# Interleaved rotary embedding: plain fp32 transfers on two queues, casts on ScalarE, tiles of eight positions

## The chip, the core and the metric

The kernel runs on one core of a Trainium2 chip. The metric is the device time of one execution in microseconds; the median of several runs is compared. A profile is one such execution with every instruction and every DMA packet recorded.

The core has several engines, each with a queue of its own that runs in order. VectorE (DVE in the profile) does elementwise work on two tensors, ScalarE (ACT) copies, casts and scales, GpSimd (POOL) is used here only to issue transfers, and SyncE (SP) issues transfers too. Data move between the memory outside (HBM) and the memory on the core (128 partitions) through 16 DMA engines. An engine that issues a transfer doesn't wait for it; whoever needs the data waits on a semaphore.

## What is computed

`x` has shape (8, 2048, 16, 64) in fp32: batch, position, head, element. Neighbouring elements form pairs, and each pair is turned by an angle that depends on the position and on the pair's place in the head:

```
x1, x2 = x[..., 0::2], x[..., 1::2]
out[..., 0::2] = x1 * cos - x2 * sin
out[..., 1::2] = x1 * sin + x2 * cos
```

`cos` and `sin` have shape (2048, 32): one value for each position and pair, the same for every batch and head. Input and output are 67.1 MB each. The arithmetic may be done in bf16.

## The kernel before

A tile holds 128 partitions x K = 4 positions x 16 heads x 64 elements, that is 4096 elements in each partition. The sequence is cut into G = 4 groups of 512 positions. Neighbouring positions lie in one partition, so each partition's part of a tile is one run of 16 KB in HBM. There are 8 batches x 4 groups = 32 tiles; the outer loop runs over groups, the inner one over batches, so that a group's tables serve eight tiles.

All tiles on the core are bf16. The transfers themselves cast: the load (L73) reads fp32 and writes bf16, and the store (L86) reads bf16 and writes fp32. Both are issued on GpSimd's queue, in program order.

The tables are loaded in fp32 by eight small transfers on SP's queue (L50, L51). For each group, `build_tables` (L53 to L64) spreads them on ScalarE to full tiles of 4096 bf16 elements: for each of the four positions one copy of cos, doubled for both elements of a pair and repeated for the 16 heads (L61), and two of sin, with a plus sign for even places (L62) and a minus sign for odd ones (L63).

For each tile VectorE then runs three operations over 4096 elements: `qt = x * s_tab` (L78), `pt = x * c_tab` (L79), and `pt = pt + swap(qt)` (L84), where the swap is done by the access pattern, which reads each pair of `qt` backwards.

A framework orders the instructions and sets the waits. `xt` has five buffers, `qt` and `pt` four each, the tables three. A load waits until VectorE has read its buffer's earlier tile; the multiply into `pt` waits until the earlier store from that buffer has landed.

Of the kernel before, what the change touches and what calls it, by code (L numbers as in the profile page):

```python
# [2 lines left out]

# [4 lines left out]


@with_exitstack  # L10
def kernel(
    ctx: ExitStack,
    tc: tile.TileContext,
    x: bass.AP,
    cos: bass.AP,
    sin: bass.AP,
    out: bass.AP,
):
    nc = tc.nc
    fp32 = mybir.dt.float32  # L20
    bf16 = mybir.dt.bfloat16
    mult = mybir.AluOpType.mult
    add = mybir.AluOpType.add

    B, S, H, D = x.shape
    P = 128
    K = 4
    G = S // (P * K)
    D2 = D // 2
    HD = H * D  # L30
    W = K * HD
    ntiles = B * G

    TAIL_SPLIT = 0

    x_t = x.rearrange("b (g p k) h d -> (b g) p (k h d)", p=P, k=K)
    out_t = out.rearrange("b (g p k) h d -> (b g) p (k h d)", p=P, k=K)
    cos_g = cos.rearrange("(g p k) c -> g p (k c)", p=P, k=K)
    sin_g = sin.rearrange("(g p k) c -> g p (k c)", p=P, k=K)

    consts = ctx.enter_context(tc.tile_pool(name="consts", bufs=1))
    tabpool = ctx.enter_context(tc.tile_pool(name="tabpool", bufs=3))
    xpool = ctx.enter_context(tc.tile_pool(name="xpool", bufs=5))
    qpool = ctx.enter_context(tc.tile_pool(name="qpool", bufs=4))
    opool = ctx.enter_context(tc.tile_pool(name="opool", bufs=4))

    cos_sb = consts.tile([P, G, K, D2], fp32)
    sin_sb = consts.tile([P, G, K, D2], fp32)
    for g in range(G):
        nc.sync.dma_start(out=cos_sb[:, g], in_=cos_g[g])  # L50
        nc.sync.dma_start(out=sin_sb[:, g], in_=sin_g[g])  # L51

    def build_tables(g):  # L53
        c_tab = tabpool.tile([P, W], bf16, name="c_tab")
        s_tab = tabpool.tile([P, W], bf16, name="s_tab")
        c_dst = c_tab.rearrange("p (k h i j) -> p k h i j", k=K, h=H, i=D2, j=2)
        s_dst = s_tab.rearrange("p (k h i j) -> p k h i j", k=K, h=H, i=D2, j=2)
        for k in range(K):
            c_src = cos_sb[:, g, k : k + 1, :].to_broadcast([P, H, D2, 2])
            s_src = sin_sb[:, g, k : k + 1, :].to_broadcast([P, H, D2])  # L60
            nc.scalar.copy(out=c_dst[:, k], in_=c_src)  # L61
            nc.scalar.copy(out=s_dst[:, k, :, :, 0], in_=s_src)  # L62
            nc.scalar.mul(out=s_dst[:, k, :, :, 1], in_=s_src, mul=-1.0)  # L63
        return c_tab, s_tab  # L64

    tile_idx = 0
    for g in range(G):
        c_tab, s_tab = build_tables(g)
        for b in range(B):
            i = b * G + g  # L70

            xt = xpool.tile([P, W], bf16)
            nc.gpsimd.dma_start(out=xt, in_=x_t[i])  # L73

            qt = qpool.tile([P, W], bf16)
            pt = opool.tile([P, W], bf16)

            nc.vector.tensor_tensor(out=qt, in0=xt, in1=s_tab, op=mult)  # L78
            nc.vector.tensor_tensor(out=pt, in0=xt, in1=c_tab, op=mult)  # L79
            q_swap = dataclasses.replace(  # L80
                qt, offset=qt.offset + 1, ap=[qt.ap[0], [2, W // 2], [-1, 2]]
            )
            pt3 = pt.rearrange("p (a j) -> p a j", a=W // 2, j=2)
            nc.vector.tensor_tensor(out=pt3, in0=pt3, in1=q_swap, op=add)  # L84

            nc.gpsimd.dma_start(out=out_t[i], in_=pt)  # L86
            tile_idx += 1


# [1 line left out]
_INS = ['x', 'cos', 'sin']  # L91
_OUTS = [((8, 2048, 16, 64), 'float32')]


# [23 lines left out]
```

## Time and profile before

| | |
|---|---|
| median of 12 runs | 323.04 us (322.67 to 323.32) |
| the profiled execution | 323.09 us |
| its span, first to last instruction | 321.3 us |
| store issues: from issue to landing, median | 12.6 us, 32 of them |
| load issues: from issue to landing, median | 22.7 us, 32 of them |
| last multiply, add and store begin | 303.2, 305.5, 308.1 us |

Busy time counts instructions that compute. The DMA row gives, for each of 40 equal slices of the span, the busy share of the 16 DMA engines in tenths; the row below it gives the bytes they moved, counted at the destination. Where a transfer casts, its source has twice or half as many bytes.

### The profile page before, as it was taken

Reading aid. Unit: us, or ns where it says so; the run is one execution under the profiler, and the core shown is the slowest. Engines: PE = TensorE matmul, PEld = TensorE weight load, DVE = VectorE, ACT = ScalarE, POOL = GpSimd, SP = SyncE. Lnnn points to the kernel's source line nnn. Section 1 sums busy time; section 2 is a strip of 40 time slices with the busy share of each in tenths; the row PEclk is TensorE's granted clock in tenths of the full one; section 3 lists DMA queues with packets and bytes.
Section 4 is the critical chain, followed back from the end, with each engine's and each line's share of the span. In section 5 each row is a group of like instructions: output and inputs, shape, how many; then the busy total and the mean of one; then the engine's idle time right before and its main releaser. Section 6 shows DMA issues by size and latency. Waiting matters only on the chain.

```text
span 321.3 us, 304 instructions
## 1 busy us (share of the span) xinstructions
DVE 213.1 (66%) x96; ACT 36.9 (11%) x49; POOL 34.4 (11%) x68
## 2 busy tenths in 40 slices
DVE  0799887601999901999900999920899920899930
ACT  8698100000820000000000000000000000000000
POOL 3010100400010030010030001030001030000100
DMA  7999999999999999999999999999999999999994
GB/s 137 214 220 214 347 329 432 424 428 249 217 215 392 428 443 255 212 212 390 433 432 262 213 219 377 428 424 286 217 217 357 426 441 289 217 212 343 445 432 169
DMA packets 10371, 101.21 MB, mean 315 GB/s; under 512 B 1153, under 2 KB 2177, under 8 KB 2177
## 3 DMA queue, kind: packets, MB, share of 16 engines
q0 software_dynamic: 9216, 100.67, 101.6%
q1 hardware_dynamic: 1152, 0.52, 0.8%
q14 instruction: 3, 0.02, 0.0%
HBM read 67.63 MB, written 67.11 MB: 419 GB/s over the span
## 4 chain that ended last, share of the span: by engine, by line
DVE 43%; DMA 32%; issue 15%; POOL 3%; ACT 2%; POOLq 0%; DVEq 0%
DMA xt<-in_x_dram 24%; DVE pt L84 17%; DVE qt L78 14%; DVE pt L79 13%; DMA out_dram<-pt 7%; POOL out_dram L86 1%; POOL xt L73 1%; ACT c_tab L61 1%; ACT s_tab L62 1%; ACT s_tab L63 1%; DMA cos_sb<-in_cos_dram 1%; POOLq L113 0%; POOLq L86 0%; DVEq L78 0%
## 5 line engine op out<-in xcount | busy, mean ns | idle before, releaser
L78 DVE TENSOR_TENSOR qt<-xt,s_tab 128x4096 bf16<-128x4096 bf16 x32 | 73.1, 2287 | 80.0 <-DMA xt<-in_x_dram 80.0
L79 DVE TENSOR_TENSOR pt<-xt,c_tab 128x4096 bf16<-128x4096 bf16 x32 | 73.1, 2286 | 14.5 <-ACT c_tab L61 10.3
L84 DVE TENSOR_TENSOR pt<-pt,qt 128x4096 bf16<-128x4096 bf16 x32 | 73.1, 2286 | 0.2
L86 POOL DMA_DIRECT2D out_dram<-pt x32 | 17.1, 534 | 260.5 <-DVE pt L84 260.5
L73 POOL DMA_DIRECT2D xt<-in_x_dram x32 | 17.2, 560 | 13.5 <-DVE qt L78 11.0
L62 ACT CAST s_tab<-sin_sb 128x512 bf16<-128x512 f32 x16 | 12.2, 762 | 52.1 <-DVE qt L78 48.1
L61 ACT CAST c_tab<-cos_sb 128x1024 bf16<-128x1024 f32 x16 | 16.2, 1022 | 0.5 <-DMA cos_sb<-in_cos_dram 0.5
L63 ACT ACTIVATE s_tab<-sin_sb 128x512 bf16<-128x512 f32 x16 | 12.2, 760 | 0.0
L61 ACT ACT_TABLE_LOAD x1 | 1.3, 1283 | 0.7 <-PEq L102 0.7
L102 POOL MEMSET const-float32-0.0<- 128x1 f32 x1 | 0.1, 98 | 0.2 <-issue 0.2
L102 POOL MEMSET const-bfloat16-1.0<- 128x1 bf16 x1 | 0.1, 101 | 0.0
L102 POOL MEMSET const-float32-1.0<- 128x1 f32 x1 | 0.1, 98 | 0.0
L102 POOL MEMSET const-uint8-127<- 128x1 uint8 x1 | 0.1, 98 | 0.0
## 6 DMA issues: line engine op xcount, KB each, us to landing
out_dram<-pt POOLq DMA_DIRECT2D x32, 2048.0 KB, 12.6
xt<-in_x_dram POOLq DMA_DIRECT2D x32, 1024.0 KB, 22.7
cos_sb<-in_cos_dram SPq DMA_DIRECT2D x4, 64.0 KB, 13.0
sin_sb<-in_sin_dram SPq DMA_DIRECT2D x4, 64.0 KB, 17.6
```

The source lines that it names most:

```text
L61: nc.scalar.copy(out=c_dst[:, k], in_=c_src)
L62: nc.scalar.copy(out=s_dst[:, k, :, :, 0], in_=s_src)
L63: nc.scalar.mul(out=s_dst[:, k, :, :, 1], in_=s_src, mul=-1.0)
L73: nc.gpsimd.dma_start(out=xt, in_=x_t[i])
L78: nc.vector.tensor_tensor(out=qt, in0=xt, in1=s_tab, op=mult)
L79: nc.vector.tensor_tensor(out=pt, in0=xt, in1=c_tab, op=mult)
L84: nc.vector.tensor_tensor(out=pt3, in0=pt3, in1=q_swap, op=add)
L86: nc.gpsimd.dma_start(out=out_t[i], in_=pt)
L102: nc = _bacc.Bacc("TRN2", target_bir_lowering=False, num_devices=1)
```

## The change

- Transfers no longer cast. `x` is loaded as fp32 on SP's queue and the result is stored as fp32 on ScalarE's queue (Activation). GpSimd has no part any more.
- K is 8, so G = 2 and there are 16 tiles of 8192 elements in each partition, 32 KB in fp32. Five such tiles (`NX`) are held. The result is written back into the tile from which x came, and the store reads it there. When the last piece of tile i has been widened, the load of tile i + 5 into the same buffer is put on SP's queue, where it waits for the store to land.
- Computing goes in pieces of four positions (4096 elements): `halve` casts a piece to bf16 on ScalarE, `rotate` does the three VectorE operations, in place where it can, and `widen` casts back to fp32 on ScalarE. `halve` runs one piece ahead of `rotate`. There are three buffers for the halved piece and one for `qt`.
- The first tile is loaded and worked in pieces of 1, 1, 2 and 4 positions, the last one in 4, 2, 1 and 1, and the last one is stored so as well.
- The tables are compact: one value for each position and element of a head, without the 16 heads. They are built once for the whole sequence, by three VectorE instructions, from two transfers in place of eight. The multiplies repeat a table row over the heads through their access pattern (a step of 0). The table transfers come after the four loads of tile 0 on SP's queue.
- The order of instructions is the program's own (`manual_schedule`).

The core of the diff:

```diff
-    K = 4
+    K = 8
+    NX = 5
...
-        nc.sync.dma_start(out=cos_sb[:, g], in_=cos_g[g])
-        nc.sync.dma_start(out=sin_sb[:, g], in_=sin_g[g])
...
-            nc.scalar.copy(out=c_dst[:, k], in_=c_src)
-            nc.scalar.copy(out=s_dst[:, k, :, :, 0], in_=s_src)
-            nc.scalar.mul(out=s_dst[:, k, :, :, 1], in_=s_src, mul=-1.0)
...
-            nc.gpsimd.dma_start(out=xt, in_=x_t[i])
-            nc.vector.tensor_tensor(out=qt, in0=xt, in1=s_tab, op=mult)
-            nc.vector.tensor_tensor(out=pt, in0=xt, in1=c_tab, op=mult)
-            nc.vector.tensor_tensor(out=pt3, in0=pt3, in1=q_swap, op=add)
-            nc.gpsimd.dma_start(out=out_t[i], in_=pt)
...
+    first_runs = [(0, 1), (1, 2), (2, 4), (4, 8)]
+    last_runs = [(0, 4), (4, 6), (6, 7), (7, 8)]
...
+    def load(i):
+        g, b = groups[i]
+        tiles[i] = xpool.tile([P, K, HD], fp32, name="xt")
+        for k0, k1 in load_runs(i):
+            nc.sync.dma_start(out=tiles[i][:, k0:k1], in_=x_t[b, g, :, k0:k1])
+
+    def halve(j):
+        i, k0, k1 = pieces[j]
+        halved[j] = hpool.tile([P, 4, HD], bf16, name="xh", bufs=3)
+        nc.scalar.copy(out=halved[j][:, : k1 - k0], in_=tiles[i][:, k0:k1])
+
+    def rotate(j):
...
+        qt = hpool.tile([P, 4, HD], bf16, name="qt")
...
+                ap=[a.ap[0], [D, nk], [0, H], [1, D]],
...
+        nc.vector.tensor_tensor(out=rows(qt), in0=rows(xh), in1=tab(s_tab), op=mult)
+        nc.vector.tensor_tensor(out=rows(xh), in0=rows(xh), in1=tab(c_tab), op=mult)
...
+        nc.vector.tensor_tensor(out=xh3, in0=xh3, in1=q_swap, op=add)
...
+    def widen(j):
+        i, k0, k1 = pieces[j]
+        nc.scalar.copy(out=tiles[i][:, k0:k1], in_=rotated.pop(j)[:, : k1 - k0])
+        g, b = groups[i]
+        for r0, r1 in store_runs(i):
+            if r1 == k1:
+                nc.scalar.dma_start(out=out_t[b, g, :, r0:r1], in_=tiles[i][:, r0:r1])
+        if k1 == K and i + NX < n:
+            load(i + NX)
+
+    with tc.manual_schedule():
+        load(0)
+        nc.sync.dma_start(out=cos_sb, in_=cos_t)
+        nc.sync.dma_start(out=sin_sb, in_=sin_t)
+        for i in range(1, NX):
+            load(i)
...
+        nc.vector.tensor_copy(out=s2[:, :, 0], in_=sin_flat)
+        nc.vector.tensor_scalar_mul(s2[:, :, 1], sin_flat, -1.0)
+        nc.vector.tensor_copy(
+            out=c_tab.rearrange("p g k (i j) -> p (g k i) j", j=2),
+            in_=cos_sb.rearrange("p g c -> p (g c)").to_broadcast([P, G * K * D2, 2]),
+        )
+        halve(0)
+        for j in range(len(pieces)):
+            if j + 1 < len(pieces):
+                halve(j + 1)
+            rotate(j)
+            widen(j)
```

## Prediction

> **What bounds the kernel now.** I read the profile's page from the top: busy times, then the 40 slices, then the DMA queues.
>
> ```profile
> span 321.3 us, 304 instructions
> DVE 213.1 (66%) x96; ACT 36.9 (11%) x49; POOL 34.4 (11%) x68
> ...
> DMA  7999999999999999999999999999999999999994
> GB/s 137 214 220 214 347 329 432 424 428 249 217 215 392 428 443 255 212 212 390 433 432 262 213 219 377 428 424 286 217 217 357 426 441 289 217 212 343 445 432 169
> ...
> q0 software_dynamic: 9216, 100.67, 101.6%
> q1 hardware_dynamic: 1152, 0.52, 0.8%
> ...
> HBM read 67.63 MB, written 67.11 MB: 419 GB/s over the span
> ```
>
> No engine is busy for more than 66% of the span, but the 16 DMA engines stand at 9 in every slice except the first and the last. The GB/s row alternates between about 216 and 430 because it counts bytes at the destination: a load reads 16 KB of fp32 per packet and writes 8 KB of bf16, a store the reverse. Counted on the wide side, both are the same. The windows view over pure stretches says so (us, busy of DVE, ACT, POOL, clock, DMA share, GB/s):
>
> ```profile
> 125.00:145.00 20.00, 16.97 (x8) 0.00 (x0) 1.08 (x2) 1.00 1.04 216
> 150.00:170.00 20.00, 11.32 (x6) 0.00 (x0) 4.25 (x8) 1.00 1.06 432
> 250.00:265.00 15.00, 9.15 (x5) 0.00 (x0) 3.71 (x7) 1.00 1.05 428
> ```
>
> Loads: 2 x 216 = 432 GB/s. Stores: 428 to 432. So the kernel is bound by moving 67.11 MB in and 67.11 MB out, 134.22 MB, and DVE's 80 us of waiting for `xt` (L78) are the other side of that. The chain of waits gives DVE 43% and DMA 32%; I don't take the DVE part for the bound, since the DMA engines run full beside it.
>
> The ends, from 0.2 us windows and the timeline:
>
> ```profile
> 1.60:1.80 0.20, 0.00 (x0) 0.20 (x1) 0.20 (x1) 1.00 0.07 20
> ...
> 2.60:2.80 0.20, 0.00 (x0) 0.20 (x1) 0.20 (x1) 1.00 4.04 348
> ...
> 316.80:317.00 0.20, 0.00 (x0) 0.00 (x0) 0.00 (x0) 1.00 0.25 82
> 317.00:317.20 0.20, 0.00 (x0) 0.00 (x0) 0.00 (x0) 1.00 0.00 0
> ```
>
> The first byte (a table) moves at about 1.75, the x loads start in earnest at 2.6, and the last 16 KB packet starts just before 317.0, so data ends about 317.5 and 3.8 us of closing follow. From 2.6 to 317.5 are 314.9 us. The table packets share that time: 0.8% of 321.3 = 2.6 us of all engines. The rest, 312.3 us, moves 134.22 MB at 429.8 GB/s. That includes the turns between loading and storing.
>
> **What the change does, part by part.**
>
> *Bytes.* fp32 loads and stores move the same 134.22 MB of HBM traffic. Since the wide side set the pace before, dropping the cast from the DMA saves nothing by itself. It doubles the bytes on the SBUF side, from half-loaded to fully loaded, which no row here shows.
>
> *Rate.* Packets go from 16 KB to 32 KB and from one queue to two. Bounds: unchanged, 429.8 GB/s, gives 134.22/429.8 = 312.3 us; the ceiling of 435.2 GB/s that the Trainium skill states ("DMA: Bandwidth & Descriptors", Where 436 GB/s comes from) gives 308.4 us. Below: a loss, next paragraph. I take 432, what pure stretches already reach: 310.7 us, a gain of **1.6 us**.
>
> The same page has a figure that speaks against the change: in its section "iDMA fabric", a plain load stream issued from SP with 4 KiB rows runs alone at 408.7 GB/s. By it the data would take 328.4 us. The case's rows show 432 with casting packets whose wide side is 16 KB. If the page's shortfall is a cost for each row (4096 B at 27.2 GB/s is 150.6 ns, at 408.7/16 it is 160.4, so some 10 ns), 32 KB rows make it less than 1%; if it belongs to uncast HWDGE streams as such, it stays. The nearer row here is the packet size, so I side with 432 and keep 408.7 for the range.
>
> *Start.* SP issues its first DMA at 0.74 before and its first byte moves at 1.75. The first thing on SP is now a load of x, so the x data start at 1.75, not 2.6: **0.85 us** gained. Each SP issue took 0.43 us (the eight table issues), and the smallest new load, 0.52 MB, takes 1.2 us to move, so issuing stays ahead.
>
> *Tables.* 1024 rows of 512 B become 512 rows of 1 KB. Below, 0.52 MB at 432 is 1.2 us; above, the 2.6 us of now. The packets are the same few nanoseconds of fixed cost each, so half of the excess of 1.4 goes with half of them: I take 1.9, **0.7 us** gained, whatever place in the queue they have.
>
> *ScalarE.* Removed: 48 table instructions (36.9 us busy with the table load). Added: 64 casts' worth, two for each half tile of 4096 elements.
>
> ```profile
> L61 ACT CAST c_tab<-cos_sb 128x1024 bf16<-128x1024 f32 x16 | 16.2, 1022 | 0.5 <-DMA cos_sb<-in_cos_dram 0.5
> L62 ACT CAST s_tab<-sin_sb 128x512 bf16<-128x512 f32 x16 | 12.2, 762 | 52.1 <-DVE qt L78 48.1
> L78 DVE TENSOR_TENSOR qt<-xt,s_tab 128x4096 bf16<-128x4096 bf16 x32 | 73.1, 2287 | 80.0 <-DMA xt<-in_x_dram 80.0
> L84 DVE TENSOR_TENSOR pt<-pt,qt 128x4096 bf16<-128x4096 bf16 x32 | 73.1, 2286 | 0.2
> ```
>
> 1024 contiguous elements take 1022 ns. Four times that is 4.1 us, an upper bound; with the fixed part of 186 ns of "ScalarE: Activation LUTs" (What ACT_TABLE_LOAD costs) taken out three times, 3.5 us, an estimate; I take 3.6. A tile of 8 positions needs four: 14.4, with one store issue of 0.45 and waits some 15.5 us. The DMA needs 2 x 4.19 MB / 432 = 19.4 us for a tile. So ScalarE has 3.9 us to spare in each tile and its casts would have to reach 4.6 us to become the bound.
>
> *VectorE.* The same three operations over the same elements, 3 x 2.2 us (the pitch in the timeline) = 6.6 for each half tile, 13.2 a tile, against 19.4. New is the table operand with a repeated 64-element row. L84 already reads its swapped operand in runs of two and takes 2286 ns like the contiguous L78, so I cost it at nothing. The three table instructions (512, 512 and 1024 fp32 elements) move to DVE: between 0.6 us each (the DVE rate of L78) and 1.2[...], about 2.5 us at the head, before the first store only.
>
> *Does the DMA queue ever run dry?* Head: five loads at 9.7 us keep the engines busy to 1.75 + 1.9 + 48.5 = 52 alone. Tables land at about 15 (four runs of tile 0 come first), table instructions to 17.5, then the four pieces of tile 0 go through halve, rotate, widen in turn: store 0 goes out at about 36. From then on loads and stores share. At half rate each, a store lands every 19.4 us (55, 75, 94, ...) and releases the load of the tile five further on; load 4 lands at about 67, when load 5 has been waiting since 57. A tile takes about 21 us from its landing to its store; five tiles x 19.4 = 97 us for a buffer's turn leave 76 for a load and a store in the queues. About two of each wait at any time, so SP's wait for a store's landing (only later loads stand behind it on SP) and the store issue behind widening on ACT (the next halve stands behind it, 0.45 us) are covered. If that cover were gone, each missing load would idle the engines for up to 9.7 us.
>
> Tail: load 15 is issued when store 10 lands, near 249, and lands near 281, with some 3.4 tiles of stores (33 us) still to move; tile 15's compute ends about 300. So stores stay queued to the end, and the last piece, 0.52 MB, is long in the queue. I keep the 3.8 us of closing.
>
> **Sum.** 1.75 + 1.9 + 310.7 + 3.8 = 318.15 us of span, 3.15 below 321.3. The profiled execution took 323.09 beside its span of 321.3, so 1.8 us lie around it: **319.9 us**. Its 323.09 is 0.05 above the median of 323.04, so no correction.
>
> **Rivals.**
>
> *Two fp32 queues move less than one casting queue* (the slower side). Place: the 270 us in which each engine alternates between 32 KB loads and stores, with SBUF's side at full load. For: no row shows it; the page's 408.7. Against: the turns between loading and storing are already inside the 429.8 and cost at most 312.3 - 310.7 = 1.6 us. Price: at 420 (the lowest 5 us windows show 419) 319.6 us, so 328.8 in all with the other 9.25; at 408.7, 337.6. It decides below 134.22/(321.3 - 1.75 - 1.9 - 3.8) = 427.7 GB/s: a loss of 0.5% against 429.8 undoes everything. Chance 0.20.
>
> *A compute engine becomes the bound.* If the repeated table row halves the DVE rate, two multiplies of 4.4 and an add of 2.2 make 11 us for each half tile, 352 us plus a head of 17.5 and a tail of about 6 with what lies around: some 377 us. L84 speaks against it; on ScalarE the 3.9 us of slack do. Chance 0.05.
>
> *No difference*: packets and queues leave the rate at 427 to 428.5, so that the head's gain is spent in the transfers: 323 us. For it: the engines are already full; against it: it is a narrow band between the two larger cases. Chance 0.07.
>
> The forecast, 319.9, has 0.68. Its own range is 316.6 (435.2 GB/s and 1 us less closing) to 322.4 (429.8 GB/s gives 321.5, and 0.9 at the ends). A measurement can tell about 0.2%, 0.65 us. The range, with about 1 in 10 left out on each side, reaches into the first rival: 316.5 to 331 (417 GB/s). Faster 0.68, same 0.07, slower 0.25.
>
> **What would show it.** The DMA row at 9 throughout; destination GB/s near 432 in every slice, where it alternated before; first x packet before 2 us; ACT some 235 us and DVE some 215 us busy, both under 75%; halved tiles of 4096 at 3.6 us; table multiplies still at 2.29 us. I am wrong if the GB/s row sits under 427.7 with the engines full, if slices fall below 9 after the head, or if either multiply takes more than 3 us.

## The result and the profile after

The changed kernel takes **318.67 us** (median of 7 runs, 318.57 to 318.83; an eighth run on record, which this median leaves out, took 319.06) against 322.96 us before (29 runs, 322.67 to 323.32). The ratio is 0.9867, 95% interval 0.9858 to 0.9876: 1.3% faster. The forecast was 319.9, 1.0% faster. The profiled execution took 318.59 us; 1.8 us lie around its span, as before.

The page of the changed kernel, first its top:

```profile
span 316.8 us, 352 instructions
DVE 223.2 (70%) x111; ACT 230.0 (73%) x73; POOL 0.2 (0%) x4
...
DMA  8999999999999999999999999999999999999997
GB/s 312 420 459 401 459 397 434 426 455 405 463 397 463 397 460 410 451 434 427 451 410 459 405 455 405 455 410 455 430 430 451 410 430 428 426 432 439 442 414 302
...
q1 hardware_dynamic: 3712, 67.63, 50.1%
q10 hardware_dynamic: 2736, 67.11, 49.1%
...
HBM read 67.63 MB, written 67.11 MB: 425 GB/s over the span
```

The DMA row is full as before, and the GB/s row no longer alternates between 216 and 430: nothing casts on the way, so source and destination have the same bytes. ScalarE went from 11% to 73% busy, and the row shows no cost of it: the DMA engines stay at 9 in all slices but the first and the last. The groups by shape of the same kernel (busy us, mean ns, idle time ahead of them):

```profile
L75 ACT CAST xh<-xt 128x4096 bf16<-128x4096 f32 x30 | 108.1, 3603 | 50.7 <-DMA xt<-in_x_dram 45.4 <-ACT xt L105 5.4
L105 ACT CAST xt<-xh 128x4096 f32<-128x4096 bf16 x30 | 108.1, 3602 | 2.1 <-DVE xh L100 1.8
L94 DVE TENSOR_TENSOR qt<-xh,s_tab 128x4096 bf16<-128x4096 bf16 x30 | 68.8, 2292 | 56.6 <-ACT xh L75 55.8
```

A cast of 4096 elements takes 3.60 us, and the multiply with a repeated table row takes 2292 ns where the full table took 2287: the repetition costs nothing that can be seen.

The two ends, in windows of 0.2 us (columns as before):

```profile
1.40:1.60 0.20, 0.00 (x0) 0.20 (x1) 0.00 (x0) 1.00 0.00 0
1.60:1.80 0.20, 0.00 (x0) 0.20 (x1) 0.00 (x0) 1.00 0.47 82
...
315.20:315.40 0.20, 0.00 (x0) 0.00 (x0) 0.00 (x0) 1.00 0.10 41
315.40:315.60 0.20, 0.00 (x0) 0.00 (x0) 0.00 (x0) 1.00 0.00 0
```

The x data start at 1.7, where before they started at 2.6. By the packet records the last packet ends at 315.55, and only **1.3 us** follow to the end of the span at 316.81. Before, the last packet ended at 317.55, and 3.8 us followed to 321.32. That closing is the largest single piece of the gain, and the prediction had kept it unchanged. It is visible in the sequencer rows, first of the kernel before, then of the changed one (instruction, count, shortest/median/longest ns, first and last start):

```profile
L113 POOLq DRAIN  x3: 40/93/12466, 308.1 to 321.1; - x3
```

```profile
L158 POOLq DRAIN  x3: 34/41/75, 0.7 to 316.6; - x3
```

Before, GpSimd's drain begins after its last store issue at 308.1 and lasts 12.5 us, to 320.6: 3.0 us past the end of the last packet. From its end to the end of the span there are another 0.8 us. In the changed kernel GpSimd has issued nothing and its longest drain takes 75 ns.

### The profile page after: what moved, and what is told of

Same layout as the page of the kernel before. It is cut to its first block, busy times and chain, and to the rows that moved or that the text cites. A ratio compares the mean times of both kernels' runs of the same rounds, so it can differ in the third digit from the quotient of the medians.

```text
span 316.8 us, 352 instructions
## 1 busy us (share of the span) xinstructions
DVE 223.2 (70%) x111; ACT 230.0 (73%) x73; POOL 0.2 (0%) x4
## 4 chain that ended last, share of the span: by engine, by line
DMA 62%; ACT 26%; DVE 4%; issue 3%; another core or an unknown queue 2%; SPq 1%; ACTq 1%
DMA xt<-in_x_dram 31%; DMA out_dram<-xt 28%; ACT xt L105 14%; ACT xh L75 12%; DMA sin_sb<-in_sin_dram 4%; DVE xh L95 1%; DVE xh L100 1%; DVE qt L94 1%; SPq L70 1%; ACTq L109 1%; DVE s_tab L121 0%; SPq L115 0%; DVE s_tab L122 0%; ACTq L105 0%
## 5 line engine op out<-in xcount | busy, mean ns | idle before, releaser
L75 ACT CAST xh<-xt 128x4096 bf16<-128x4096 f32 (+2 forms) x36 | 116.1, 3224 | 66.8 <-DMA xt<-in_x_dram 61.4
L105 ACT CAST xt<-xh 128x4096 f32<-128x4096 bf16 (+2 forms) x36 | 116.0, 3223 | 14.7 <-DVE xh L100 14.4
L94 DVE TENSOR_TENSOR qt<-xh,s_tab 128x4096 bf16<-128x4096 bf16 (+2 forms) x36 | 74.0, 2055 | 71.2 <-ACT xh L75 70.3
L100 DVE TENSOR_TENSOR xh<-xh,qt 128x4096 bf16<-128x4096 bf16 (+2 forms) x36 | 74.0, 2055 | 1.2
L95 DVE TENSOR_TENSOR xh<-xh,c_tab 128x4096 bf16<-128x4096 bf16 (+2 forms) x36 | 74.0, 2055 | 1.2
L123 DVE CAST c_tab<-cos_sb 128x1024 bf16<-128x1024 f32 x1 | 0.7, 684 | 0.0
```

The costliest lines, as they stand in the source:

```text
L75: nc.scalar.copy(out=halved[j][:, : k1 - k0], in_=tiles[i][:, k0:k1])
L94: nc.vector.tensor_tensor(out=rows(qt), in0=rows(xh), in1=tab(s_tab), op=mult)
L95: nc.vector.tensor_tensor(out=rows(xh), in0=rows(xh), in1=tab(c_tab), op=mult)
L100: nc.vector.tensor_tensor(out=xh3, in0=xh3, in1=q_swap, op=add)
L105: nc.scalar.copy(out=tiles[i][:, k0:k1], in_=rotated.pop(j)[:, : k1 - k0])
L123: nc.vector.tensor_copy(out=c_tab.rearrange("p g k (i j) -> p (g k i) j", j=2), in_=cos_sb.rearrange("p g c -> p (g c)").to_broadcast([P, ...
```

## The experiments

All compute the whole result. "Closing" is the time from the end of the last packet to the end of the span.

**1. Who makes the closing: the last store on GpSimd's queue.**

```diff
-                nc.scalar.dma_start(out=out_t[b, g, :, r0:r1], in_=tiles[i][:, r0:r1])
+                eng = nc.gpsimd if i == n - 1 and r1 == K else nc.scalar
+                eng.dma_start(out=out_t[b, g, :, r0:r1], in_=tiles[i][:, r0:r1])
```

> The changed kernel with only its very last store (512 KB) issued from GpSimd's queue in place of ScalarE's. Theory A (the changed kernel gained 2.5 us because its last data are followed by 1.3 us of closing where the kernel before needed 3.8, and that belongs to a last store from GpSimd's queue): 321 to 322 us, closing 3.5 to 4.5 us. Theory B (the closing belongs to the use of GpSimd's queue anywhere in the kernel): the same here, 321 to 322. Theory C (the prediction's: the closing is no part of it, the gain is in the rate): 318.7 within 0.5.

Measured: 318.79 us (318.64 to 319.64), closing 1.2 us. That a last store from GpSimd's queue makes the long closing by itself has fallen. Its drain ended 0.4 us after its last packet; in the kernel before it was 3.0 us. What differs is how much was issued there: 1 transfer against 64.

**2. The table loads on GpSimd's queue.**

```diff
-        nc.sync.dma_start(out=cos_sb, in_=cos_t)
-        nc.sync.dma_start(out=sin_sb, in_=sin_t)
+        nc.gpsimd.dma_start(out=cos_sb, in_=cos_t)
+        nc.gpsimd.dma_start(out=sin_sb, in_=sin_t)
```

> The changed kernel with only its two table loads issued from GpSimd's queue, at the head. Theory A (last store decides the closing): 318.7 within 0.5, closing near 1.3 us. Theory B (any use of the queue): 321 to 322, closing near 3.8. Theory C: 318.7 within 0.5.

Measured: 320.70 us (319.51 to 321.02), closing 1.3. The closing is short, so mere use of the queue doesn't make it long. But the time missed all three expectations. In its profile (319.5 us) the transfers ran dry near the end: 0.56 of the DMA engines' time from 312 to 313 and 0.13 from 314 to 315, because the last piece was widened only by 314.1 (by 312.3 in the changed kernel). Experiment 5 is on why it is so late.

**3. All x loads on GpSimd's queue.**

```diff
-            nc.sync.dma_start(out=tiles[i][:, k0:k1], in_=x_t[b, g, :, k0:k1])
+            nc.gpsimd.dma_start(out=tiles[i][:, k0:k1], in_=x_t[b, g, :, k0:k1])
```

> The changed kernel with all its x loads issued from GpSimd's queue, stores still from ScalarE's. In the kernel before, GpSimd's closing drain ended 2.7 us after the last landing with 64 transfers issued there, in the one with 8 positions 1.3 us with 32, and 0.1 us with 1. Theory A (the drain costs some 0.04 us for each transfer issued on that queue, and it only shows when the queue's last transfer is the kernel's last): closing 1.1 to 1.4 us as in the changed kernel, time 318.7 to 320.0 (the loads start up to 0.9 us later). Rival (any use of that queue costs the long closing): 321 or more. The rate in the middle stays at 433 if the queue that issues makes no difference.

Measured: 326.47 us (326.25 to 326.97), closing 1.4. On the closing the theory holds: 22 transfers were issued on GpSimd, and its drain was over at 317.5, before the last store packets ended at 323.2, so nothing shows at the end. From the end of the last packet of GpSimd's queue to the end of its drain it took 0.4 us with 1 transfer, 0.6 with 2 (experiment 2), 1.3 with 22, 1.8 with 32 (experiment 7) and 3.0 with 64: about 0.4 us and **0.04 us for each transfer**. The 22 here don't cast, the 32 and the 64 do, so the cast isn't the cause. Nearly every transfer has 144 packets here, so it may be the packets that are counted. On the rate the expectation was wrong. First this kernel, then the changed one:

```profile
60.00:260.00 200.00, 139.34 (x61) 143.76 (x42) 6.83 (x13) 1.00 1.00 426
```

```profile
60.00:260.00 200.00, 145.90 (x64) 150.34 (x43) 0.00 (x0) 1.00 1.01 434
```

With loads on GpSimd's queue beside stores on ScalarE's, the full engines moved 426 in place of 434 GB/s. By the packet records of this window it is the loads that lose: a 32 KB load packet took 1253 ns in the mean against 1214 in the changed kernel, with the same median of 1213, as 151 of 1296 took over 1.3 us; a store packet took 1216 against 1213. Why stays open, and so does how much of it GpSimd's queue makes. A rival is not ruled out: as the loads start late here, the tables are the first to move, and in experiment 6 that order alone brings the window to 431.

**4. What the packet size is worth: tiles of 4 positions.** First with ten tiles held, the same bytes; then with six.

```diff
-    K = 8
+    K = 4
-    NX = 5
+    NX = 10
-    first_runs = [(0, 1), (1, 2), (2, 4), (4, 8)]
-    last_runs = [(0, 4), (4, 6), (6, 7), (7, 8)]
+    first_runs = [(0, 1), (1, 2), (2, 4)]
+    last_runs = [(0, 2), (2, 3), (3, 4)]
-        runs = first_runs if i == 0 else last_runs if i == n - 1 else [(0, 4), (4, 8)]
+        runs = first_runs if i == 0 else last_runs if i == n - 1 else [(0, K)]
```

> The changed kernel with tiles of 4 positions (16 KB packets) and ten tiles held, so that the same bytes are held. In the trace of the changed kernel plain packets of 4, 8, 16 and 32 KB take 159, 309, 611 and 1213 ns, that is 8.4 ns on top of 27.2 GB/s whatever their size. Theory A (fixed cost of a packet): 4096 more packets over 16 engines x 8.4 ns = 2.2 us more, 320.6 to 321.2. Rival (packets overlap as the casting ones of before did, so their size is worth nothing): 318.7 within 0.5. A tile of half the size also means twice the waits; if those starved the queues the DMA row would fall below 9.

Measured: 329.93 us (329.88 to 329.97), slower than the kernel before. The middle says what the packets cost, the end says something else. The window from 60 to 260 us, and the DMA row:

```profile
60.00:260.00 200.00, 129.28 (x57) 130.12 (x37) 0.00 (x0) 1.00 1.01 431
```

```profile
DMA  7999999999999999999999999999999999977678
```

431 GB/s against 434 in the changed kernel: the engines are as full, and packets of 16 KB carry some 0.5% less (431.1 against 433.1 when a packet that lies across an edge of the window counts by its share). But after 290 us they run dry. The waits of this kernel name a cause that has nothing to do with packets:

```profile
ACT xh L75 <- DMA out_dram<-xt: 18.2, 4, 12.3
```

A halving, which needs loaded data only, sat behind a store issue. In the trace all transfers share eight semaphores, loads and stores alike, and a store that is held goes out within 0.1 us of the landing of the transfer that had its semaphore before. The store issued at 234.76 has the semaphore of a store that landed at 234.68. The next one, whose cast had ended at 242.3, has that of a load issued at 234.74; the load landed at 263.65, and the store went out at 263.72. With six tiles held (`NX = 6`):

> Tiles of 4 positions as in the run with ten held, but only six held. That run took 329.9 us: its middle ran at 431 GB/s, but from 290 us on its DMA row fell to 5 to 8, because ScalarE's store issues waited for a transfer semaphore (there are eight, taken in turn, and with ten loads ahead the one whose turn it is belongs to a load still queued), and the halving behind them waited too. Theory A (shared semaphores): with fewer loads ahead the waits go and the time is 320.0 to 321.0, which is the packets' price alone. Rival (half tiles as such are too small to keep the queues filled): 325 or more with the DMA row below 9 at the end.

Measured: 320.28 us (320.21 to 320.31), the DMA row at 9 to the end, and the wait for `out_dram` gone. So holding fewer tiles is some 9.6 us faster, and half tiles cost 1.6 us against 318.67. About 0.3 us of this is the tables, whose rows halve with the tile: 1024 packets of 28.6 ns against 512 of 46.8, over 16 engines.

**5. Why the last tile lands so late: load it whole.** The timeline of the changed kernel shows when its runs landed (start, length, what, and in brackets how long the engine waited and for what):

```profile
287.94 1.90 ACT L75 CAST xh<-xt 128x2048 bf16<-128x2048 f32 x1 [1.93 <-DMA xt<-in_x_dram]
...
298.87 1.04 ACT L75 CAST xh<-xt 128x1024 bf16<-128x1024 f32 x1 [5.53 <-DMA xt<-in_x_dram]
...
307.97 1.04 ACT L75 CAST xh<-xt 128x1024 bf16<-128x1024 f32 x1 [6.25 <-DMA xt<-in_x_dram]
```

```diff
-        return first_runs if i == 0 else last_runs if i == n - 1 else [(0, K)]
+        return first_runs if i == 0 else [(0, K)]
```

> The changed kernel with the last tile loaded as one transfer (32 KB packets) in place of runs of 4, 2, 1 and 1 positions; its compute and stores stay in pieces. In the changed kernel the four runs landed at about 288, 299 and 308 us, where 281 had been predicted. Theory A (the DMA engines take one packet from each queue in turn, so packets of 16, 8 and 4 KB get 1/3, 1/5 and 1/9 of the rate beside stores of 32 KB): the whole tile lands by 295, the stores stay queued to the end, and the time is 318.0 to 318.6. Rival (the loads are late because the store before them landed late; the size of the packets doesn't matter): the landing stays at 300 or later, and the time is 319 or more, since no piece can start early.

Measured: **318.42 us** (318.23 to 318.52; the changed kernel 318.57 to 318.83), the lowest median here, 0.25 us below the changed kernel's. That difference is not clear of the noise: against the kernel before, the ratios are 0.9846 to 0.9872 here and 0.9858 to 0.9876 there. What is clear is the landing. The first piece of the last tile now waits for the whole of it, and still:

```profile
281.60 3.60 ACT L75 CAST xh<-xt 128x4096 bf16<-128x4096 f32 x1 [4.76 <-DMA xt<-in_x_dram]
```

The whole tile is there at 281.6, 26 us ahead of the last run of the version in pieces. The packet records of the changed kernel fit one packet from each queue in turn, so that a 4 KB packet waits for a store packet of 32 KB each time. The tile before landed at 260.0 us (median of its 16 closing packets), the runs of 4, 2 and 1 positions at 274.5, 286.7 and 297.6. So 2.10, 1.05 and 0.52 MB took 14.5, 12.2 and 10.9 us, that is 145, 86 and 48 GB/s: 1/3, 1/5 and 1/9 of 433. Cutting the last load so that the tail starts early made it start late. It cost little, because 30 us of stores were queued; in experiment 2 pieces that came 1.8 us later left the engines dry.

**6. The head: tables first, tile 0 whole.** A version with both edits on top of experiment 5, then each alone.

```diff
-        load(0)
         nc.sync.dma_start(out=cos_sb, in_=cos_t)
         nc.sync.dma_start(out=sin_sb, in_=sin_t)
+        load(0)
...
-        return first_runs if i == 0 else [(0, K)]
+        return [(0, K)]
```

> The changed kernel with the tables loaded first and the first and last tile loaded as one transfer each. 704 packets fewer in the loads at 8.4 ns over 16 engines are 0.4 us; the tables' place moves no bytes. Theory (only bytes, packets and the two ends count): 317.9 to 318.5, first store some 8 us earlier. Rival (the small first runs are needed to get going): 319 or more, with the DMA row below 9 in the first slices.

Measured: 321.11 us (320.40 to 323.97). Wrong: slower, and with a spread that no kernel above shows.

> The kernel with the last tile loaded whole (318.4 us), with one more edit: the table loads stand ahead of tile 0 on SP's queue, tile 0 still in four runs. The version that had both this and tile 0 loaded whole took 321.1 us with a spread of 3.6 us between its runs, and its 16 DMA engines ended up to 2 us apart. Theory A (the tables at the very start make the loss): 320 to 322 with a wide spread. Rival (loading tile 0 in one piece makes it): 318.2 to 319.

Measured: 326.39 us (325.27 to 327.63), worse than both expectations.

> The kernel with the last tile loaded whole, with tile 0 loaded whole as well and the tables behind it. Theory A (the tables at the very start made the loss of the version with both): 318.0 to 318.6, 384 packets fewer being worth 0.2 us. Rival (tile 0 in one piece made it): 320 or more with a wide spread.

Measured: 318.64 us (318.36 to 318.88). So the tables' place makes the loss: 8.0 us with tile 0 in runs, 2.5 us with tile 0 whole (321.11 against 318.64). The runs of tile 0 alone make no clear difference (318.42 and 318.64), but behind the tables they go with 5.3 us more. The DMA row of the version with the tables first:

```profile
DMA  7999999999999999999999999999999999995995
```

It drops in the slice from about 292 to 300. Each transfer ends with 16 packets of 4 bytes, as many as there are DMA engines, so the time between the first and the last of them shows how far apart the engines are. In this version the last loaded tile's lie between 281.9 and 292.3 us, in the version of experiment 5 between 279.2 and 281.2: some engine had fallen some 10 us behind, and the waiting tile held up the rest. The lag was not all made at the start. It was 3.0 us when tile 0 had landed, 5.3 at the fourth tile and grew from there to 10.4; in experiment 5 it was 0.5, 1.9 and 2.0. In the two versions with the tables first, single table packets of 1 KB took up to 313 and 516 ns. Behind tile 0 none took more than 61 in the changed kernel and in experiment 5, but one took 195 in experiment 1, which lost next to nothing. What makes an engine fall behind is open.

**7. 32 KB packets in the kernel before, still casting.**

```diff
-    K = 4
+    K = 8
-    tabpool = ctx.enter_context(tc.tile_pool(name="tabpool", bufs=3))
+    tabpool = ctx.enter_context(tc.tile_pool(name="tabpool", bufs=1))
-    qpool = ctx.enter_context(tc.tile_pool(name="qpool", bufs=4))
-    opool = ctx.enter_context(tc.tile_pool(name="opool", bufs=4))
+    qpool = ctx.enter_context(tc.tile_pool(name="qpool", bufs=1))
+    opool = ctx.enter_context(tc.tile_pool(name="opool", bufs=3))
```

> The kernel before with tiles of 8 positions (32 KB on the wide side), still casting in the transfers on GpSimd's queue; one buffer for each table and for qt, three for pt. Theory A (casting packets of 16 KB overlap each other, so their fixed cost is mostly hidden): 322.0 to 323.3. Rival (as in the prediction, the packet size brings the rate from 429.8 to 432 or more): 320.5 to 321.5. If the single buffers starve the queue, the DMA row drops below 9 and the run says nothing on the packets.

Measured: 327.86 us (327.52 to 328.18). As a whole it says nothing on packets, since the queue starved. The busy rows of VectorE and DMA show where:

```profile
DVE  0069996009999930098998299920098899199910
...
DMA  8999999999969699999999999999999999999996
```

The two slices with 6 lie at 90 to 98 and 106 to 114 us. VectorE is full there, and its stores go out 13.1 us apart (82.1, 95.3 and 108.4), where one store takes 9.7 at 433 GB/s; the next loads were issued only at 117.8, behind these stores in GpSimd's order. It isn't the single table buffers: the second group's tables are built from 153 to 172 us, and VectorE waits 1.5 us for them. Where it didn't starve it does. Counting bytes of the wide side from the packet records in full stretches (200 to 250 us after the first load packet): before 431.3 GB/s, this kernel 433.1, the changed kernel 433.2, tiles of 4 positions 431.3. In these four kernels the packet size goes with the rate; with or without a cast in the transfer, on one queue or two, it is the same. So the expectation that casting packets hide their cost was wrong.

**8. How many tiles must be held.** `NX = 3` and `NX = 2` in place of 5.

> The changed kernel with three tiles held in place of five. A tile takes some 21 us from its landing to its store; three tiles at 19.4 us each leave 37 us for a load and a store in the queues, which take 9.7 us each alone and 19.4 each when they share. Theory (the bytes set the time as long as a transfer is queued): just covered, 319 to 323, with the DMA row at 8 or 9. Rival (cover is lost as soon as less than one load waits behind the one that runs): 326 or more.

> The same with two tiles held. A buffer's turn is then load 9.7 + compute 21 + store 9.7 + some 3 us of waits, 43 us for two tiles, against 38.8 us of transfers: the buffers become the bound. Theory: 16 tiles x 21.7 us, 345 to 360 us with the DMA row at 7 to 9. Rival (load and store of the two tiles never overlap fully, so each turn is longer): 365 or more.

Measured: 366.90 us (366.02 to 369.50) and 483.23 us (482.65 to 483.68). Both are far above my estimates, on the rivals' side, so something in the turn of a buffer was missing from them. The timeline with two tiles shows it:

```profile
259.26 2.29 DVE L100 TENSOR_TENSOR xh<-xh,qt 128x4096 bf16<-128x4096 bf16 x1
274.00 3.60 ACT L75 CAST xh<-xt 128x4096 bf16<-128x4096 f32 x1 [15.92 <-DMA xt<-in_x_dram]
```

The last piece of a tile is rotated by 261.6, but ScalarE's next instruction is the halving of the next tile's first piece (halve runs one ahead), and that waits until 274.0 for its load. Only then comes the widening, and only then the store. So a tile's store can't go out before the next tile has landed. With two tiles, load and store therefore never overlap: a turn takes some 31 us (219.19 and 250.59 are the store issues), and 16 of them would be 496. By the packet records both queues are at work at once for 0 us with two tiles, 90 with three and 194 with five. No run widens before it halves, so what that order would give isn't known. With five tiles the same wait is there, 61.4 us of `ACT xh L75` waiting for `xt` in the changed kernel, but other stores are queued behind which it is hidden.

## The prediction, point by point

The direction and the time were right. The mechanism was right in part: the bytes are the bound and the rate rose, but the largest piece of the gain, the closing, stood at nothing in the sum. That the time still came within 1.3 us is partly luck: 1.4 us that no term had forecast were lost outside the full stretches.

| term of the gain in span | predicted | measured |
|---|---|---|
| start of the x data | 0.85 | 0.9 (2.6 to 1.7) |
| tables | 0.7 | 1.1 (2.6 before; 512 packets of 46.8 ns over 16 engines are 1.5) |
| rate in full stretches | 1.6 | 1.4 (134.22 MB at 433.0 against 431.1 GB/s) |
| closing | 0 | 2.5 (3.8 to 1.3) |
| all | 3.15 | 4.5 (321.3 to 316.8) |

The measured terms add up to 5.9, 1.4 more than the span shows. The other 1.4 us went back in the transfers outside the full stretches, for the most part in the head; the windows of the changed kernel:

```profile
0.00:20.00 20.00, 5.42 (x9) 5.56 (x5) 0.20 (x4) 1.00 0.96 393
20.00:60.00 40.00, 36.55 (x18) 37.33 (x13) 0.00 (x0) 1.00 0.99 419
60.00:260.00 200.00, 145.90 (x64) 150.34 (x43) 0.00 (x0) 1.00 1.01 434
```

This view counts a packet where it starts. Counted by shares, the changed kernel moves 408 GB/s up to 20 us, where tile 0's small packets and the tables go, 408 again from 36 to 46 us and 433 behind that. At 36 to 46 us the first stores begin, and 18 of 80 load packets took over 1.3 us, up to 1.86; why is open.

- **Bytes, not engines, are the bound**: right. With ScalarE and VectorE at 73% and 70% the DMA row stays at 9. The casts came out at 3.60 us for the 3.6 taken: 1024, 2048 and 4096 elements took 1044, 1896 and 3603 ns, that is 0.83 ns for each element and a fixed part of some 190 ns, where 186 had been taken.
- **Rate**: the size of the term held, its working only in part. 429.8 was an average that held head and turns, and I set it against 432, which I took for the rate that pure stretches already had. Like for like it is 431.1 against 433.0, and experiments 4 and 7 show that packet size makes this. It stays below the ceiling of 435.2 that the prediction took. The 408.7 GB/s of the load stream with 4 KiB rows in the Trainium skill ("DMA: Bandwidth & Descriptors", iDMA fabric) is close to what such rows give here: plain packets of 4, 8, 16 and 32 KB took 159, 309, 611 and 1213 ns in this trace, that is 8.4 ns each on top of 27.2 GB/s, and a stream of 159 ns for 4096 B on 16 engines would be 412 GB/s, an estimate. To side with 432 was right, for the reason given. From 16 to 32 KB the measured rate rises by less than these times say, 0.5 and not 0.7%.
- **Closing**: the step that failed. "I keep the 3.8 us of closing" gave no reason why it should stay. Its length, 3.8 us, was read rightly. Experiments 1, 2, 3 and 7 show that GpSimd's drain makes it, 0.04 us for each transfer issued there, 3.0 us past the last packet for 64; the changed kernel issues none there, and 1.3 us are left.
- **Tail**: "lands near 281" was wrong for the version with the last load in runs (308) and right for the whole load (281.6). I had shared the rate by halves, and the landings fit a share by packets.
- **Cover**: "the next halve stands behind it" saw what waits behind a store, not what a store waits behind. Five tiles hid it; experiment 8 shows what it costs with two and three.
- **Tables in any place**: wrong for the very first place on the queue (experiment 6).
- **Rivals**: two fp32 queues on SP and ScalarE lose no rate, 433 against 431; no compute engine became the bound.

## What to carry to other kernels

Where all DMA engines are full, look for what is left in the packets (fixed nanoseconds each), in the first and last microseconds, and in the drain of the queue that issued the transfers; the busy shares of the compute engines didn't tell of any of these here. When two queues share the engines, a load in small packets can be held back by stores in large ones, so cutting the last load fine can delay it. In an engine that runs in order, an instruction put ahead to prefetch also holds back what comes after it: count the buffers with that wait in the turn.

## What was not expected of the hardware

GpSimd's closing drain grew with the transfers issued there: 0.4, 0.6, 1.3, 1.8 and 3.0 us past its last packet for 1, 2, 22, 32 and 64 of them. Loads issued by GpSimd beside stores issued by ScalarE moved 426 GB/s, against 434 with SP's loads, though there the tables also moved first. And one order of the same transfers, the two small table loads ahead of everything, cost 8 us (326.39 against 318.42), with the DMA engines ending the last load up to 10 us apart.
